# First expert layer: row products of the gathered tile spread otherwise over the routing stage, and the u products drawn out past the gates

## The chip, the core and the metric

One core of a Trainium2 chip runs the whole program in one launch. Its engines work side by side, each through its own queue of instructions in order: TensorE (PE), VectorE (DVE), ScalarE (ACT), GpSimd (POOL) and SyncE (SP, which here issues transfers only). Semaphores order them among each other. The metric is the device time of one execution in microseconds (us).

## The reference

Two blocks of two layers each. The change touches one place, the expert sublayer (`peer`) of layer 0 of the first block, which runs over 512 tokens (256 of the context, 256 of the latent sequence) with 1024 channels. There are 16384 experts, each a row of `u_tab` and a row of `v_tab`; a token uses 16 of them for each of 8 heads:

```
qry = (xb @ w_query).reshape(P, 8, 2, 128)
s = einsum('phcd,hckd->phck', qry, sub_keys)
top_s, top_i = top_k(s, 16)
cand_s = top_s[..., 0, :, None] + top_s[..., 1, None, :]      # 256 candidates of a head
best_s, pos = top_k(cand_s, 16)
gate = softmax(best_s)
act = gelu(einsum('pd,phkd->phk', xb, u_tab[idx]))
out = einsum('phk,phkd->pd', gate * act, v_tab[idx])
```

So for each token 128 rows of u are multiplied with the token's activations, and 128 rows of v are added up with the weights that come out.

## The kernel before, in words

The 512 tokens are four tiles of 128, and two ways of computing are mixed. **The chosen tile** (tile 0, class `Chosen`) does what the formula says: a step gathers one row of u for each of its 128 tokens (an indirect DMA on POOL, line 1295, 128 rows of 4 KB into one of four buffers `ch_r`) and DVE multiplies it with the token's activations and adds up (line 1311, one instruction and a short one that reads the sum). There are 128 such steps, here called row products, and later 128 more with rows of v (lines 1320 and 1322, `ch_y`). **The three dense tiles** (384 tokens, class `Experts`) multiply with every expert instead: 128 blocks of 128 experts, here called u products 0 to 127. For one block SP loads 0.5 MB of u (a transfer of 1 MB serves two blocks), ACT rounds it to `peer_uh` (line 1210), DVE takes the rest to `peer_ul` (line 1211), PE multiplies 24 times (lines 154 to 156), ACT applies the Gelu (line 1225) and the result is written to memory (`act_dram`). Experts that a token didn't choose get the gate 0. For that each dense tile makes a table of gates (`peer_gates`): for four tokens at a time ACT makes one-hots of the first key (lines 1171 and 1173), DVE one-hots of the second key times the gate (line 1180, four instructions, ten buffers), PE multiplies the two (line 1183) and ACT copies the result out (line 1184); every 32 tokens a block of it is written to memory (`g_dram`, line 1187). After that come the v products: SP loads gates (`gtile`) and activations, DVE and ACT make `coefh` and `coefl` and split v (`peer_vh`, `peer_vl`), PE multiplies.

Before its gates or its row products a tile goes through the router (`peer_route`): PE scores, and DVE's searches for the largest 16, then six operations of 128 x 2048 elements (`eq` and `key`).

The order of all this is set in three layers. `merge` runs several generators beside each other by a clock that each advances by the numbers it yields; `to(us, gen, own)` scales a generator so that it takes `us` in all; a u product advances its clock by `pace`. `routing()` is the list of stretches: router 0, then router 1 beside row products, then the gates of a dense tile beside the next router and row products, twice, then the last gates beside row products. The order in which the generators run is not yet the program's: a scheduler of the language orders each engine's instructions once more by its own estimate of durations, and keeps the order that `issue_after` (`K.behind`) asks for: instructions of the same engine in such a block come behind the one named. All buffers come from pools in which the next user waits for the last reader. The gathers' queue on POOL holds nothing else in this stage.

Of the kernel before, what the change touches and what calls it, by code (L numbers as in the profile page):

```python
# [1147 lines left out]
def peer_gates(K, pool, stage, t, route, g_d, scalar):  # L1148
# [3 lines left out]
    nc = K.nc  # L1152
# [11 lines left out]
    for c in range(128 // GT):  # L1164
        st = stage([128, 128, GT], c)
        for q in range(GT // 4):
# [10 lines left out]
            p = K.bank("v")  # L1177
            for k in range(4):
                o2 = pool.tile([128, 128], F32, name="oh2", tag="oh2", bufs=10)
                nc.vector.scalar_tensor_tensor(  # L1180
                    o2, K.iota, k2T[:, tk + k:tk + k + 1], gT[:, tk + k:tk + k + 1].to_broadcast([128, 128]),
                    op0=OP.is_equal, op1=OP.mult)
                nc.tensor.matmul(p[:, k * 128:(k + 1) * 128], o1[:, k], o2, start=True, stop=True)  # L1183
# [751 lines left out]
SEG = (1, 1, 0, 0)  # L1935
# [106 lines left out]
def peer_layer(K, A, tc, i, hT, hp, tag, nt, x, gate, ahead, pace, done, side=None, begin=None, chosen=0):  # L2042
# [5 lines left out]
    nc = K.nc  # L2048
    ntt = nt // 128
    spare = ntt == 2  # L2050
    dense = list(range(chosen, ntt))
    nd = nt - 128 * chosen
    g_d = K.dram.tile([nd // GT, 128, 128, GT], F32, name=f"g_dram{i}")
    act_d = K.dram.tile([ahead, 128, nd], F32, name=f"act_dram{i}")
    q_d = [K.dram.tile([128, 16, 128], F32, name=f"q_dram{i}{t}") for t in range(ntt)]
    with ExitStack() as c:
# [6 lines left out]
        with ExitStack() as c2:  # L2063
# [8 lines left out]
            gp = c2.enter_context(tc.tile_pool(name="gp", bufs=1, reuse_waits="tile"))  # L2072
            route = [[] for _ in range(ntt)]
# [18 lines left out]
            def to(us, gen, own):  # L2092
                return slow(gen, us / own)

            def rows(n, us):

                return to(us, (next(chs[0].go) for _ in range(n)), 1.7 * n)

            def gated(n):
                return peer_gates(K, gp, stage, n, route[dense[n]], g_d, chosen > 0)  # L2100

            def routing():
                if chosen:
                    yield from to(32, router(0), 73)
                    yield from merge(to(52, router(1), 73), rows(16, 52))
                    yield from merge(to(142, gated(0), 83), to(142, router(2), 73), rows(36, 142))
                    yield from merge(to(142, gated(1), 83), to(142, router(3), 73), rows(36, 142))
                    yield from merge(to(115, gated(2), 83), rows(40, 115))
                    return
                yield from router(0)  # L2110
                yield from merge(gated(0), router(1))
                yield from gated(1)
# [44 lines left out]
def program(ctx, tc, A, out):  # L2157
# [18 lines left out]
    with ExitStack() as c0:  # L2176
# [34 lines left out]
        late.close()  # L2211
        K.raw = raw
        N = Norm(K, None, x, lambda: hp.tile([128, 8, 512], F32, name="nxT", tag="plo", bufs=1))
        peer_layer(K, A, tc, 0, hT, hp, "ph", 512, x, SEG, 128, 3.77, N.raw, chosen=1)

        xl = x[2:4]
        h2 = hp.tile([128, 2, 8, 256], F32R, name="qhl", tag="ph", bufs=1)
# [198 lines left out]
```

## Time and profile before

| | |
|---|---|
| time, median of 3 runs | 4038.18 us (4034.49 to 4052.68) |
| the profiled execution's own time | 4038.09 us |
| its span | 4036.3 us |
| PE busy | 3756.6 us, 93% |
| DVE busy | 3067.0 us, 76% |
| ACT busy | 2110.7 us, 52% |
| POOL busy | 968.9 us, 24% |

The span runs from the first to the last instruction; what lies around it is the launch. A matmul counts as busy from its start to a modelled end, so a busy PE may still be slowed by its clock, which the profile gives as the share of full speed that was granted. The stage of the change, from the first u product to the first v product, lies between 985 and 1711 us.

### The profile page before, as it was taken

To read this page: it belongs to the slowest core of one execution; us is meant where nothing else is said; L and a number is where in the kernel's file an instruction comes from. 1 tells how busy PE (TensorE), PEld (TensorE's weight loads), DVE (VectorE), ACT (ScalarE), POOL (GpSimd) and SP (SyncE) were. 2 spreads that over 40 slices of the span, in tenths; PEclk is the share of its full clock that TensorE was granted. 3 is DMA by queue.
4 is the path that set the end of the run, shared out by engine and by line. 5 is a ranking of instruction groups with operands and counts; after the bars stand their busy time and mean duration, and the time that the engine had idled before them with its cause. 6 is when DMAs were issued, how large, how long until landed. Compare 5 with 4: busy or idle time off the path is not lost.

```text
span 4036.3 us, 61300 instructions
## 1 busy us (share of the span) xinstructions
PE 3756.6 (93%) x22031; PEld 3263.8 (81%) x22031; DVE 3067.0 (76%) x6258; ACT 2110.7 (52%) x3676; POOL 968.9 (24%) x1040
## 2 busy tenths in 40 slices
PE   7988987999999999899999889999999999988899
PEld 6868765788989899888888779999887768963697
DVE  6997578542999995487888757996677766859785
ACT  5545665533358677633333455665456545640364
POOL 1473255210144430033333300000000030115210
PEclk9999998999999999999999999999999989989999
DMA  4432554634599894699998247677689953542354
GB/s 175 159 115 87 165 175 152 199 133 161 200 322 337 316 346 176 221 386 358 353 355 315 97 141 242 234 255 260 229 303 315 327 178 126 182 172 84 127 188 157
DMA packets 359770, 890.37 MB, mean 221 GB/s; under 512 B 32568, under 2 KB 227752, under 8 KB 300584
## 3 DMA queue, kind: packets, MB, share of 16 engines
q1 hardware_dynamic: 237040, 614.87, 44.5%
q10 hardware_dynamic: 85560, 137.34, 9.3%
q0 software_dynamic: 36864, 134.23, 9.0%
q8 instruction: 173, 2.83, 0.3%
q14 instruction: 133, 1.09, 0.1%
HBM read 763.94 MB, written 122.39 MB: 220 GB/s over the span
## 4 chain that ended last, share of the span: by engine, by line
PE 58%; DVE 21%; DMA 11%; ACT 4%; issue 4%; POOL 3%; ACTq 0%; DVEq 0%; SPq 0%; POOLq 0%
PE ps_a L156 5%; PE ps_a L154 5%; PE ps_a L155 5%; PE ps_v L155 5%; PE ps_v L154 5%; PE ps_v L156 5%; PE ps_mm L155 3%; PE ps_mm L154 3%; PE ps_mm L156 3%; DMA act<-act_dram 3%; DMA ch_r<-in_peer_u_rows_dram,ch_i 3%; PE ps_v L1183 2%; DVE peer_ul L1211 2%; DMA wraw<-in_peer_v_dram 2%; DVE ch_r L1311 2%
## 5 line engine op out<-in xcount | busy, mean ns | idle before, releaser
L139 DVE TENSOR_TENSOR wlo<-wraw,whi 128x1024 fp32r<-128x1024 f32 x320 | 395.6, 1242 | 275.5 <-ACT whi L138 274.0
L155 PE MATMUL ps_v<-peer_vl,coefh 128*128 128x512 f32 x1280 | 501.9, 392 | 12.6 <-DVE peer_vl L1211 12.3
L154 PE MATMUL ps_v<-peer_vh,coefh 128*128 128x512 f32 x1280 | 491.8, 391 | 17.6 <-ACT coefh L1255 15.8
L138 ACT ACTIVATE whi<-wraw 128x1024 fp32r<-128x1024 f32 x324 | 340.7, 1058 | 316.2 <-PE ps_mm L155 73.8
L156 PE MATMUL ps_v<-peer_vh,coefl 128*128 128x512 f32 x1280 | 441.7, 390 | 0.0
L1210 ACT ACTIVATE peer_vh<-wraw 128x1024 fp32r<-128x1024 f32 x256 | 261.5, 1053 | 276.5 <-DMA wraw<-in_peer_v_dram 141.8
L1211 DVE TENSOR_TENSOR peer_vl<-wraw,peer_vh 128x1024 fp32r<-128x1024 f32 x256 | 306.7, 1222 | 121.5 <-ACT peer_vh L1210 121.4
L1210 ACT ACTIVATE peer_uh<-wraw 128x1024 fp32r<-128x1024 f32 x256 | 269.0, 1058 | 248.3 <-PE ps_a L155 184.9
L156 PE MATMUL ps_a<-ph,peer_ul 128*128 128x384 f32 x1024 | 354.7, 348 | 27.6 <-DVE peer_ul L1211 27.4
L1211 DVE TENSOR_TENSOR peer_ul<-wraw,peer_uh 128x1024 fp32r<-128x1024 f32 x256 | 311.5, 1223 | 79.9 <-ACT peer_uh L1210 78.4
L154 PE MATMUL ps_a<-ph,peer_uh 128*128 128x384 f32 x1024 | 355.0, 347 | 8.1 <-ACT peer_uh L1210 8.1
L155 PE MATMUL ps_a<-plo,peer_uh 128*128 128x384 f32 x1024 | 348.2, 340 | 0.0
L1295 POOL DMA_INDIRECT ch_r<-in_peer_v_dram,ch_i x128 | 198.7, 1552 | 506.9 <-DVE ch_y L1320 292.6
L155 PEld LDWEIGHTS ps_v<-peer_vl,coefh 128*128 128x128 f32 x1280 | 240.9, 188 | 68.7 <-DVE peer_vl L1211 19.4
L154 PEld LDWEIGHTS ps_v<-peer_vh,coefh 128*128 128x128 f32 x1280 | 240.4, 188 | 69.2 <-ACT coefh L1255 16.1
L154 PE MATMUL ps_a<-qhl,peer_uh 128*128 128x256 f32 x1024 | 290.3, 284 | 1.0 <-ACT act L1225 0.6
L156 PE MATMUL ps_a<-qhl,peer_ul 128*128 128x256 f32 x1024 | 289.0, 283 | 2.1 <-DVE peer_ul L1211 2.1
L155 PE MATMUL ps_a<-qhl,peer_uh 128*128 128x256 f32 x1024 | 289.2, 283 | 0.0
L1295 POOL DMA_INDIRECT ch_r<-in_peer_u_rows_dram,ch_i x128 | 184.1, 1438 | 406.1 <-DVE rep L1070 202.7
L156 PEld LDWEIGHTS ps_v<-peer_vh,coefl 128*128 128x128 f32 x1280 | 240.0, 188 | 48.8
L1180 DVE SCALAR_TENSOR_TENSOR oh<-iota,k2T,gT 128x128 f32<-128x128 f32 x640 | 192.8, 352 | 76.2 <-PE ps_v L1183 75.8
L156 PEld LDWEIGHTS ps_a<-ph,peer_ul 128*128 128x128 f32 x1024 | 196.4, 192 | 36.9 <-DVE peer_ul L1211 36.5
(681 smaller groups left out, 10348.0 us busy)
## 6 DMA issues: line engine op xcount, KB each, us to landing
wraw<-in_peer_u_dram SPq DMA_DIRECT2D x128, 1024.0 KB
wraw<-in_peer_v_dram SPq DMA_DIRECT2D x128, 1024.0 KB
wraw<-in_ffn_w_up_dram SPq DMA_DIRECT2D x44, 1024.0 KB
g_dram<-gst ACTq DMA_DIRECT2D x20, 2048.0 KB
ada_w<-in_ada_w_dram SPq DMA_DIRECT2D x136, 256.0 KB
wraw<-in_dn_w_in_dram SPq DMA_DIRECT2D x24, 1024.0 KB
act_dram<-act ACTq DMA_DIRECT2D x128, 192.0 KB
act<-act_dram SPq DMA_DIRECT2D x128, 192.0 KB
```

Of the source, the lines that this page charges most:

```text
L138: nc.scalar.activation(hi[:, :n], r, AF.Copy)
L139: (sub or nc.vector).tensor_tensor(lo[:, :n], r, f32v(hi[:, :n]), op=OP.subtract)
L154: nc.tensor.matmul(out, ah, bh, start=start, stop=False)
L155: nc.tensor.matmul(out, ah, bl, start=False, stop=False)
L156: nc.tensor.matmul(out, al, bh, start=False, stop=stop)
L1180: nc.vector.scalar_tensor_tensor(o2, K.iota, k2T[:, tk + k:tk + k + 1], gT[:, tk + k:tk + k + 1].to_broadcast([128, 128]), op0=OP.is_equal ...
L1183: nc.tensor.matmul(p[:, k * 128:(k + 1) * 128], o1[:, k], o2, start=True, stop=True)
L1210: nc.scalar.activation(hi, r, AF.Copy)
L1211: nc.vector.tensor_tensor(lo, r, f32v(hi), op=OP.subtract)
L1295: self.K.nc.gpsimd.indirect_dma_start(out=r, out_offset=None, in_=table, in_offset=bass.IndirectOffsetOnAxis(ap=self.idx[:, c:c + 1], axis=0))
L1311: nc.vector.tensor_tensor_reduce(out=r, in0=r, in1=self.h, scale=1.0, scalar=0.0, op0=OP.mult, op1=OP.add, accum_out=dots[:, c:c + 1])
```

## The change

Three things. The row products are dealt out otherwise over the stretches of `routing()`: 16, 36, 36 and 40 of them before (128 in all), 8, 26, 26 and 68 after. While gates are made, each row product is put behind the last one-hot on DVE that the gates' generator had made (`K.one_hot`, `K.gone`, `K.behind`); that binds DVE's instruction, not the gather on POOL. And a u product advances its generator's clock by 3.95 instead of 3.77 (units of that clock, not times); the five stretches of the routing add up to 483 of them, 128 u products to 483 before and to 506 after, so that some six of them come behind the end of the gates.

```diff
--- before.py
+++ after.py
@@ -1177,7 +1177,7 @@
             p = K.bank("v")
             for k in range(4):
                 o2 = pool.tile([128, 128], F32, name="oh2", tag="oh2", bufs=10)
-                nc.vector.scalar_tensor_tensor(
+                K.one_hot = nc.vector.scalar_tensor_tensor(
                     o2, K.iota, k2T[:, tk + k:tk + k + 1], gT[:, tk + k:tk + k + 1].to_broadcast([128, 128]),
                     op0=OP.is_equal, op1=OP.mult)
                 nc.tensor.matmul(p[:, k * 128:(k + 1) * 128], o1[:, k], o2, start=True, stop=True)
@@ -2094,18 +2094,27 @@
 
             def rows(n, us):
 
-                return to(us, (next(chs[0].go) for _ in range(n)), 1.7 * n)
+                def gen():
+                    for _ in range(n):
+                        with K.behind(*K.gone):
+                            w = next(chs[0].go)
+                        yield w
+                return to(us, gen(), 1.7 * n)
 
             def gated(n):
-                return peer_gates(K, gp, stage, n, route[dense[n]], g_d, chosen > 0)
+                for w in peer_gates(K, gp, stage, n, route[dense[n]], g_d, chosen > 0):
+                    K.gone = (K.one_hot,)
+                    yield w
+
+            K.gone = ()
 
             def routing():
                 if chosen:
                     yield from to(32, router(0), 73)
-                    yield from merge(to(52, router(1), 73), rows(16, 52))
-                    yield from merge(to(142, gated(0), 83), to(142, router(2), 73), rows(36, 142))
-                    yield from merge(to(142, gated(1), 83), to(142, router(3), 73), rows(36, 142))
-                    yield from merge(to(115, gated(2), 83), rows(40, 115))
+                    yield from merge(to(52, router(1), 73), rows(8, 52))
+                    yield from merge(to(142, gated(0), 83), to(142, router(2), 73), rows(26, 142))
+                    yield from merge(to(142, gated(1), 83), to(142, router(3), 73), rows(26, 142))
+                    yield from merge(to(115, gated(2), 83), rows(68, 115))
                     return
                 yield from router(0)
                 yield from merge(gated(0), router(1))
@@ -2211,7 +2220,7 @@
         late.close()
         K.raw = raw
         N = Norm(K, None, x, lambda: hp.tile([128, 8, 512], F32, name="nxT", tag="plo", bufs=1))
-        peer_layer(K, A, tc, 0, hT, hp, "ph", 512, x, SEG, 128, 3.77, N.raw, chosen=1)
+        peer_layer(K, A, tc, 0, hT, hp, "ph", 512, x, SEG, 128, 3.95, N.raw, chosen=1)
 
         xl = x[2:4]
         h2 = hp.tile([128, 2, 8, 256], F32R, name="qhl", tag="ph", bufs=1)
```

Where that puts the instructions, at three places. First DVE's queue in the middle of the last gates, around u product 102 (`peer_ul` is one u product's splitting, `oh` a one-hot, the two rows with `ch_d` one row product). Before:

```order
L1211 TENSOR_TENSOR peer_ul<-wraw,peer_uh 128x1024
L1180 SCALAR_TENSOR_TENSOR oh_15942<-iota,k2T,gT 128x128
L1180 SCALAR_TENSOR_TENSOR oh_15988<-iota,k2T,gT 128x128
L1180 SCALAR_TENSOR_TENSOR oh_15991<-iota,k2T,gT 128x128
L1180 SCALAR_TENSOR_TENSOR oh_15994<-iota,k2T,gT 128x128
L1211 TENSOR_TENSOR peer_ul<-wraw,peer_uh 128x1024
L1180 SCALAR_TENSOR_TENSOR oh_15997<-iota,k2T,gT 128x128
L1180 SCALAR_TENSOR_TENSOR oh_16050<-iota,k2T,gT 128x128
L1180 SCALAR_TENSOR_TENSOR oh_16053<-iota,k2T,gT 128x128
L1180 SCALAR_TENSOR_TENSOR oh_16056<-iota,k2T,gT 128x128
L1211 TENSOR_TENSOR peer_ul<-wraw,peer_uh 128x1024
```

After:

```order
L1211 TENSOR_TENSOR peer_ul<-wraw,peer_uh 128x1024
L1311 ISA ch_r,ch_d<-ch_r,ch_h 128x1024
L1311 ISA ch_d 128x1
L1211 TENSOR_TENSOR peer_ul<-wraw,peer_uh 128x1024
L1311 ISA ch_r,ch_d<-ch_r,ch_h 128x1024
L1311 ISA ch_d 128x1
L1211 TENSOR_TENSOR peer_ul<-wraw,peer_uh 128x1024
L1311 ISA ch_r,ch_d<-ch_r,ch_h 128x1024
L1311 ISA ch_d 128x1
L1180 SCALAR_TENSOR_TENSOR oh_16170<-iota,k2T,gT 128x128
L1311 ISA ch_r,ch_d<-ch_r,ch_h 128x1024
L1311 ISA ch_d 128x1
```

Where four one-hots stood between two u products, row products now stand too. Over the stage, counted on DVE between the `peer_ul` of u products 0, 20, 32, 88 and 127, the row products are 1, 19, 105 and 3 before (all 128 are done by product 127), and 0, 10, 50 and 63 after, with 5 more behind product 127. The one-hots there are 0, 0, 256 and 128 before, 0, 10, 246 and 128 after, and the routers' large operations 6, 4, 8 and 6 before, 6, 6, 12 and 0 after. The last one-hot stands ahead of `peer_ul` of product 127 before and of product 119 after.

Second, DVE's queue at the end of the stage, from the last two u products on (`ch_y` are the row products with v, `peer_vl` the splitting of v). Before:

```order
L1211 TENSOR_TENSOR peer_ul<-wraw,peer_uh 128x1024 x2
L1322 TENSOR_SCALAR ch_y<-ch_r,ch_d 128x1024
L1320 SCALAR_TENSOR_TENSOR ch_y<-ch_r,ch_d,ch_y 128x1024
L1211 TENSOR_TENSOR peer_vl<-wraw,peer_vh 128x1024 x2
L1320 SCALAR_TENSOR_TENSOR ch_y<-ch_r,ch_d,ch_y 128x1024
L1211 TENSOR_TENSOR peer_vl<-wraw,peer_vh 128x1024 x2
L1320 SCALAR_TENSOR_TENSOR ch_y<-ch_r,ch_d,ch_y 128x1024
L1252 TENSOR_TENSOR act<-act,gtile 128x384 x3
L1256 TENSOR_TENSOR coefl<-act,coefh 128x384 x3
```

After:

```order
L1211 TENSOR_TENSOR peer_ul<-wraw,peer_uh 128x1024 x2
L1211 TENSOR_TENSOR peer_vl<-wraw,peer_vh 128x1024
L1311 ISA ch_r,ch_d<-ch_r,ch_h 128x1024
L1311 ISA ch_d 128x1
L1211 TENSOR_TENSOR peer_vl<-wraw,peer_vh 128x1024
L1311 ISA ch_r,ch_d<-ch_r,ch_h 128x1024
L1311 ISA ch_d 128x1
L1311 ISA ch_r,ch_d<-ch_r,ch_h 128x1024
L1311 ISA ch_d 128x1
L1311 ISA ch_r,ch_d<-ch_r,ch_h 128x1024
L1311 ISA ch_d 128x1
L1252 TENSOR_TENSOR act<-act,gtile 128x384
```

Four of the last five row products now stand between the last u product and the first `act`, out of which the first coefficients are made.

Third, ACT's queue there (`g_dram` is the write of the last block of gates, `gate` a load that ACT issues for the end of the layer, `ch_d` the Gelu over all 128 row products). Before:

```order
L1225 ACTIVATE act<-ps_a 128x384
L1227 DMA act_dram_9320<-act 128x384
L1184 ACTIVATE gst<-ps_v 128x4x128
L1187 DMA g_dram_9319<-gst 128x4096
L1225 ACTIVATE act<-ps_a 128x384
L1227 DMA act_dram_9320<-act 128x384
L1225 ACTIVATE act<-ps_a 128x384
L1961 DMA gate<-ada_rows_146 128x1024
L1227 DMA act_dram_9320<-act 128x384
L1961 DMA gate<-ada_rows_146 128x1024
L1210 ACTIVATE peer_vh<-wraw 128x1024 x4
L1255 ACTIVATE coefh<-act 128x384 x4
```

After:

```order
L1210 ACTIVATE peer_uh<-wraw 128x1024 x2
L1210 ACTIVATE peer_vh<-wraw 128x1024
L1225 ACTIVATE act<-ps_a 128x384
L1210 ACTIVATE peer_vh<-wraw 128x1024
L1227 DMA act_dram_9320<-act 128x384
L1225 ACTIVATE act<-ps_a 128x384
L1961 DMA gate<-ada_rows_146 128x1024
L1227 DMA act_dram_9320<-act 128x384
L1961 DMA gate<-ada_rows_146 128x1024
L1210 ACTIVATE peer_vh<-wraw 128x1024 x2
L1255 ACTIVATE coefh<-act 128x384
L1314 ACTIVATE ch_d<-ch_d 128x128
```

The last write of gates is no longer among the last u products, two of the four first `peer_vh` stand ahead of the last Gelu, and the Gelu over the row products stands behind the first `coefh`; before it stood far ahead.

## Rows read from the trace of the kernel before

**Rows 1.** The stage cut in five: busy time of each engine, clock, DMA.

```profile
core 0: us, PE busy (x) PEld busy (x) DVE busy (x) ACT busy (x) POOL busy (x), PEclk, DMA share, GB/s
985.00:1094.00 109.00, 101.45 (x604) 98.83 (x602) 86.97 (x368) 39.45 (x56) 6.28 (x5) 0.99 0.54 188
1094.00:1153.00 59.00, 54.68 (x290) 52.22 (x290) 55.82 (x135) 19.54 (x28) 23.69 (x19) 0.95 0.89 308
1153.00:1491.00 338.00, 314.43 (x1921) 304.20 (x1922) 324.67 (x896) 250.25 (x506) 155.08 (x106) 0.97 0.90 330
1491.00:1695.00 204.00, 200.02 (x1222) 197.88 (x1220) 108.77 (x241) 144.86 (x275) 3.58 (x3) 0.98 0.54 198
1695.00:1711.00 16.00, 0.21 (x3) 0.03 (x1) 9.91 (x10) 4.98 (x7) 7.49 (x4) 0.67 0.99 354
```

**Rows 2.** What PE waited for, 1085 to 1711 us: total, times, longest.

```profile
PE ps_a L156 <- DVE peer_ul L1211: 23.2, 21, 3.7
PE ps_v L154 <- ACT coefh L1255: 15.8, 1, 15.8
PE ps_a L154 <- ACT peer_uh L1210: 8.1, 11, 1.9
```

**Rows 3.** Pieces of the chain: start, length in us up to the next.

```profile
1205.64 2.27 DVE peer_ul L1211 x2
...
1377.90 1.05 DVE oh L1180 x4
...
1394.38 1.14 DVE ch_r L1311
...
1506.35 2.20 DVE eq L1135
...
1689.07 11.69 DMA g_dram<-gst
```

**Rows 4.** Timeline where PE never waits: start, length in us, instruction.

```profile
1681.86 1.23 DVE L1211 TENSOR_TENSOR peer_ul<-wraw,peer_uh 128x1024 fp32r<-128x1024 f32 x1 [3.57 <-ACT peer_uh L1210]
...
1682.85 0.34 PE L155 MATMUL ps_a<-plo,peer_uh 128*128 128x384 f32 x1
...
1685.80 0.33 PE L154 MATMUL ps_a<-ph,peer_uh 128*128 128x384 f32 x1
...
1686.91 1.23 DVE L1211 TENSOR_TENSOR peer_ul<-wraw,peer_uh 128x1024 fp32r<-128x1024 f32 x1 [3.83 <-ACT peer_uh L1210]
```

**Rows 5.** One stretch in which PE never waits, columns as in rows 1.

```profile
1550.00:1600.00 50.00, 50.00 (x321) 50.00 (x320) 23.24 (x52) 41.44 (x81) 0.00 (x0) 1.00 0.51 182
```

**Rows 6.** Groups by line, 1153 to 1491 us: busy, mean ns, idle before.

```profile
L1295 POOL DMA_INDIRECT ch_r<-in_peer_u_rows_dram,ch_i x105 | 154.7, 1474 | 182.1 <-DVE ch_d L1311 75.8 <-DVE oh L1180 53.1 <-DVE rep L1070 12.4
...
L1311 DVE CUSTOM_DVE_ANT_0 ch_r<-ch_r,ch_h 128x1024 f32<-128x1024 f32 x105 | 126.7, 1222 | 13.3 <-DMA ch_r<-in_peer_u_rows_dram,ch_i 13.3
```

**Rows 7.** Tile ch_r, 1153 to 1491 us: POOL min, median, max; landings.

```profile
L1295 POOL DMA_INDIRECT ch_r<-in_peer_u_rows_dram,ch_i x105: 939/1360/3931, 1152.4 to 1484.5; - x105
...
DMA to landing us min/median/max: 4.3/7.0/15.8
```

**Rows 8.** DMA queue of the gathers, 985 to 1711 us: packets, MB, share.

```profile
q0 software_dynamic: 19237, 70.09, 27.4%
```

**Rows 9.** The other DMA queues, 1491 to 1695 us.

```profile
q1 hardware_dynamic: 3044, 21.27, 29.9%
q10 hardware_dynamic: 6360, 16.65, 21.0%
```

**Rows 10.** All DMA in the v products that follow, 1711 to 2204 us.

```profile
DMA packets 91370, 177.85 MB, mean 361 GB/s; under 512 B 5456, under 2 KB 67743, under 8 KB 83402
```

**Rows 11.** Group of the one-hots, 1491 to 1695 us, columns as in rows 6.

```profile
L1180 DVE SCALAR_TENSOR_TENSOR oh<-iota,k2T,gT 128x128 f32<-128x128 f32 x128 | 38.4, 348 | 72.9 <-PE ps_v L1183 72.9
```

**Rows 12.** Timeline of ACT at the change from u to v products.

```profile
1697.79 3.89 ACT L1210 ACTIVATE peer_vh<-wraw 128x1024 fp32r<-128x1024 f32 x4 [2.08 <-issue]
1710.40 0.99 ACT L1255 ACTIVATE coefh<-act 128x384 fp32r<-128x384 f32 x2 [8.72 <-DVE act L1252]
```

## Prediction

> **What bounds the kernel now.** I read the stage in which the change lies, 985 to 1711 us, in this order. First the busy time of each engine, cut where DVE has finished `peer_ul` of u products 20, 32 and 88, and at the end of PE's last u product [rows 1]. The reader is to see DVE at 325 of 338 us in the third stretch and PE at 200 of 204 us in the fourth: the bound moves from DVE to PE. All row products but one lie in the stretches in which DVE is the bound; in the fourth DVE works 109 of 204 us. Second, what PE waits for [rows 2]: 23.2 us for `peer_ul`, 8.1 us for `peer_uh`, and once 15.8 us, between the last u product and the first v product. Third, the chain that ended last, for the steps on DVE and for that last wait [rows 3]: the last block of gates is written to memory in 11.69 us from 1689, and only then can the gates be loaded. The stage could be better packed by some 45 us at most, 1.1% of the whole.
>
> The profiled execution took 4038.09 us around a span of 4036.3 us, and the median of the runs is 4038.18; I sum against 4038.1 and shift nothing.
>
> **Prices.** On DVE a step is its distance to the next: a row product 1.14 us, `peer_ul` 1.135, a one-hot 0.26, a router's large operation 2.2 [rows 3]. On PE a u product is 24 matmuls; 17 of them take 2.95 us where PE never waits, so 4.16 us for 24, and a u product with four one-hots takes 5.05, so 0.89 us for a group of four one-hots [rows 4].
>
> **Part 1: row products leave the third stretch (1153 to 1491).** By the counts in the section on the change, 55 of 105 row products leave it (55 x 1.14 = 63 us less on DVE) and ten one-hots (2.6 us); four large router operations come in earlier (8.8 us) with some 5 us of small ones around them. DVE's work falls from 324.7 to 273 us. PE's does not fall: 56 u products x 4.16 = 233 us, 62 groups of one-hots x 0.89 = 55 us, and some 7 us of router matmuls and transposes (an estimate from a price like the one-hots'), 295 us. ACT is busy 250 us now [rows 1] and keeps its work. So PE takes over as the bound, from 338 to something over 295 us. What is late next is PE's own pace. Its clock in this stretch was 0.97 of full speed, where it is 1.00 in a stretch without waits [rows 1, 5]. At 0.97 the 295 us are 304. Three more for short waits: the three engines stay close together, and DVE, when it was the bound, needed 338 us for 325 of work. I take 307, so 31 us less. Bounds: 295 (full clock, no wait) and 326 (7% lost on the 304, nearly twice the 4% that DVE loses now on its 325).
>
> The Trainium skill, on the page "TensorE: Matmul & The Clock Gate", section "A second HAM failure mode: psum-queue depth-cycling", says that a PE which idles briefly and often between groups of matmuls keeps switching between its clock's levels. The third stretch agrees with it, at 0.97 with short waits of the kind in [rows 2]; by that rule the 304 stand as long as any short waits are left, and without it the whole would be 3991.
>
> **Part 2: the first two stretches.** The first keeps its work but for one row product: 109 us, nothing gained (bounds 107 and 109). In the second (59 us) nine row products leave (10.3 us on DVE), ten one-hots (2.6) and two large router operations (4.4) come: 3.3 us less on DVE, which was busy 55.8 of 59. PE needs 12 x 4.16 + 3 groups, 53 us. I take 57, 2 us less (bounds 55 and 59).
>
> **Part 3: the row products arrive in the fourth stretch (1491 to 1695).** It gets 63, and two of the five behind the last u product, where three were: 65 gathers and some 65 x 1.14 = 74 us more on DVE, and loses the last router's large operations (6 x 2.2 = 13 us) and some 6 us around them. DVE goes from 109 to 164 us of 204. That stays hidden if it comes evenly. Behind a row product stand the one-hots and `peer_ul`, and for these PE waits; ahead of it now stands a one-hot, which waits for PE (72.9 us of such waits for 128 one-hots, harmless now [rows 11]). Gathers: POOL takes 1.47 us for one [rows 6], a landing 7.0 us in the middle [rows 7], the product 1.22 [rows 6], and there are four buffers: (1.47 + 7.0 + 1.22) / 4 = 2.4 us a row, where the stretch leaves 204 / 68 = 3.0. With the longest landing, 15.8 us [rows 7], it is 4.6. The DMA engines: the other queues were busy 29.9% and 21.0% of 204 us [rows 9], 104 us; the gathers' queue moved 70.09 MB, 134 gathers of 0.524 MB, in 27.4% of 726 us [rows 8], 1.49 us each; 104 + 65 x 1.49 = 200 us of 204. In bytes, 198 GB/s x 204 us [rows 1] plus 65 x 0.524 less the 1.6 MB of three gathers of v makes 73 MB, 358 GB/s. The v products hold 361 GB/s over 493 us [rows 10]. So DMA comes to the rate that it can hold, with little over. I take 208 us, 4 more than before. Bounds: 198 (PE's 40 x 4.16 + 33 x 0.89 us and its edges) and 250 (3.7 us a row, half way to the worst landing).
>
> **Part 4: six u products outlast the gates.** The last write of gates now leaves eight u products, over 33 us, before the end of the stretch, so its 11.69 us [rows 3] are hidden behind them. What is late next is ACT. Its queue at this place holds the last Gelu, two issues of `gate`, two `peer_vh`, then the first `coefh`. Before, ACT went on at 1697.79, 2.6 us after PE's end at 1695.2, and four `peer_vh` took 3.89 us [rows 12]; two are left: 2.6 + 1.95 + 0.5 for `coefh` (0.99 for two [rows 12]) is 5 us. On DVE six steps of 1.14 stand between the last `peer_ul` and the first `act`; `peer_ul` ended 7 us before PE [rows 4, 12], so the two come out together if the last gathers have landed. The second `coefh` now stands behind the Gelu over all row products, and that behind the last of them; the first v product covers this with some 4 us of matmuls. I take a wait of 7 us where 15.8 was: 9 us less (bounds 0 and 15 less).
>
> The v products themselves keep their work, and I leave them at their time; DVE's row products with v start a few us later. The scheduler also orders a few instructions of the attention layer and of later stages otherwise; I count that as 0, give or take 3.
>
> **Sum.** 0 - 2 - 31 + 4 - 9 = -38: 4038.1 - 38 = 4000 us.
>
> **The rivals.**
>
> *A, PE never waits.* The third stretch at 295 (-43), the fourth at 198 (-6), the last wait 1 us (-15), the second -2: 3972. For it: a stretch at clock 1.00 without any wait exists [rows 5]. Against it: DVE there had half its time free.
>
> *B, the gathers don't keep up in the fourth stretch.* DMA at its limit makes a landing 11 us long in the mean; 13.7 us over four buffers are 3.4 us a row, 65 x 3.4 = 221 us: 17 more than before. -2 - 31 + 17 - 6 (the tail of the row products is late for the v products too) = -22: 4016. For it: 200 of 204 us of DMA. Against it: 361 GB/s can be held [rows 10].
>
> *C, the change doesn't do what it says.* The third stretch is held up by the coupling of one-hots between ACT, DVE and PE and not by DVE's sum: 326 instead of 338 (-12), the fourth +4, the last wait -9, the second -2: 4019. For it: three engines at 250, 273 and 295 us. Against it: before, PE's waits are nearly all for `peer_ul` [rows 2].
>
> *D, slower.* The mechanism of B, at its far end: each row product that waits for its gather holds up the `peer_ul` behind it, and PE. The gains elsewhere are 42 us. The fourth stretch gives them all back at 246 us, 3.8 us a row, a mean landing of 12.5 us; at 13.7 us (4.1 a row, 267 us) the kernel is 21 us slower, 4059. With all landings at 15.8, 65 x 4.6 = 299, it would be 4091. For it: 15.8 us did occur at a DMA share of 0.90. Against it: the middle was 7.0 there [rows 1, 7].
>
> **How the numbers follow.** About 0.5% of the time, 20 us, can be told from no change. Chances: the forecast (3984 to 4014) 0.53, A 0.12, B 0.15, C 0.12, D 0.08. The likeliest is 4000. Faster than 4018: the forecast, A and a third of B's spread, 0.70 together; within 4018 to 4058: the rest of B and C, and D where it only gives the gain back, 0.23; slower 0.07. The range leaves out the far half of A and of D and a little of C: 3974 to 4034.
>
> **What the changed profile would show.** Right: PE busy and not DVE closest to the length of the third stretch, which shortens by some 30 us, and waits for `peer_ul` well under 23.2 us; DVE near 165 us and DMA near 1.0 in the fourth, which is as long as before; a wait of 5 to 9 us before the first v product, ended by `coefh`, with the last write of gates long done. Wrong: waits of DVE for gathers far over the 13.3 us of [rows 6], PE waiting for `peer_ul` in the fourth stretch (B, D); PE waiting for one-hots in the third (C); or a wait of 15 us still ahead of the first v product, then for a gather or for the Gelu over the row products.

## The result and the profile after

The changed kernel takes 3981.32 us in the median of 4 runs (3979.0 to 3982.66), beside 4036.7 for the kernel before: a ratio of 0.9861, 95% interval [0.9847, 0.9876]. The profiled execution took 3981.17 us around a span of 3979.4, 56.9 us less than the one of before. The forecast was 4000 with a range from 3974 to 4034: the sign and the range held, and the gain was half as large again as the 38 us of the sum. The 3981.32 lies 3 us below the span that the forecast itself was given (3984 to 4014) and 7 us above the lower end of the range. Between the profiled executions 51.9 of the 56.9 us lie in the stage of the change.

The stage cut at the same places as in [rows 1] (columns as there):

```profile
982.00:1084.00 102.00, 98.97 (x592) 96.65 (x591) 84.10 (x359) 38.03 (x54) 1.43 (x2) 1.00 0.51 175
1084.00:1141.00 57.00, 55.77 (x330) 55.01 (x328) 55.27 (x140) 26.52 (x43) 14.67 (x13) 1.00 0.78 281
1141.00:1434.50 293.50, 293.50 (x1891) 293.04 (x1890) 276.18 (x837) 249.34 (x499) 70.29 (x50) 1.00 0.79 284
1434.50:1645.30 210.80, 202.84 (x1229) 198.94 (x1227) 153.38 (x294) 138.36 (x267) 84.18 (x63) 0.99 0.93 346
1645.30:1656.10 10.80, 0.00 (x0) 0.00 (x0) 8.00 (x12) 5.29 (x7) 4.46 (x3) 0.67 0.86 300
```

The reader is to see the third row. PE is busy for the whole 293.50 us, at a clock of 1.00: the stretch was 338 us long, with DVE at its limit and the clock at 0.97. The next row shows the price, DMA at 0.93 and PE short of the stretch by 8 us. What PE waits for, 1075 to 1657 us, in the form of [rows 2]:

```profile
PE ps_v L154 <- ACT coefh L1255: 10.8, 1, 10.8
PE ps_a L154 <- ACT peer_uh L1210: 5.9, 9, 2.1
PE ps_a L156 <- DVE peer_ul L1211: 3.3, 5, 1.0
```

23.2 us of waits for `peer_ul` have become 3.3. DVE's own waits, first in the third stretch, then in the fourth up to the first v product:

```profile
DVE peer_ul L1211 <- ACT peer_uh L1210: 9.7, 10, 3.3
...
DVE ch_r L1311 <- DMA ch_r<-in_peer_u_rows_dram,ch_i: 21.1, 13, 4.1
DVE peer_ul L1211 <- ACT peer_uh L1210: 19.0, 10, 3.3
DVE oh L1180 <- PE ps_v L1183: 10.3, 9, 2.4
DVE peer_vl L1211 <- ACT peer_vh L1210: 9.7, 1, 9.7
```

And ACT's in the third:

```profile
ACT peer_uh L1210 <- PE ps_a L155: 36.0, 24, 3.4
```

In the third stretch the 13.3 us of waits for gathers of [rows 6] are gone, and DVE now waits for ACT, which waits for PE: PE sets the pace. In the fourth DVE waits 21.1 us for gathers. The tile `ch_r` there, beside [rows 7]:

```profile
L1295 POOL DMA_INDIRECT ch_r<-in_peer_u_rows_dram,ch_i x64: 939/1081/1990, 1437.0 to 1650.7; - x64
...
DMA to landing us min/median/max: 5.0/7.8/14.9
```

And the end of the stage: the writes of gates (their issue on ACT's queue), then ACT's and DVE's timelines from the last u products on.

```profile
L1187 ACTq DMA_DIRECT2D g_dram<-gst x2: 326/326/327, 1570.7 to 1612.3; - x2
```

```profile
1647.02 1.06 ACT L1210 ACTIVATE peer_vh<-wraw 128x1024 fp32r<-128x1024 f32 x1 [10.05 <-DMA wraw<-in_peer_v_dram]
...
1655.55 0.52 ACT L1255 ACTIVATE coefh<-act 128x384 fp32r<-128x384 f32 x1 [2.88 <-DVE act L1252]
```

```profile
1636.05 2.36 DVE L1211 TENSOR_TENSOR peer_ul<-wraw,peer_uh 128x1024 fp32r<-128x1024 f32 x2 [1.55 <-ACT peer_uh L1210]
1648.10 1.22 DVE L1211 TENSOR_TENSOR peer_vl<-wraw,peer_vh 128x1024 fp32r<-128x1024 f32 x1 [9.69 <-ACT peer_vh L1210]
...
1654.96 0.55 DVE L1252 TENSOR_TENSOR act<-act,gtile 128x384 f32<-128x384 f32 x1
```

The last write of gates is issued at 1612.3, 33 us ahead of PE's last u product: the 11.69 us of [rows 3] are hidden, as forecast. Late in its place is the first load of v. SP issued it only at 1630.86, ACT's first `peer_vh` waited 10.05 us for it, and DVE, with nothing but `peer_vl` next in its queue, stood 9.7 us. Its row products and the first `act` came behind that.

### The profile page after: what moved, and what is told of

It reads as the page before. It is cut to its first block, busy times and chain, and to the rows that moved or that the text cites. A ratio compares the mean times of both kernels' runs of the same rounds, so it can differ in the third digit from the quotient of the medians.

```text
span 3979.4 us, 61280 instructions
## 1 busy us (share of the span) xinstructions
PE 3729.4 (94%) x22031; PEld 3243.2 (82%) x22031; DVE 3065.4 (77%) x6258; ACT 2107.4 (53%) x3676; POOL 975.9 (25%) x1040
## 5 line engine op out<-in xcount | busy, mean ns | idle before, releaser
L156 PE MATMUL ps_v<-peer_vh,coefl 128*128 128x512 f32 x1280 | 402.3, 391 | 0.0
L1295 POOL DMA_INDIRECT ch_r<-in_peer_u_rows_dram,ch_i x128 | 172.3, 1346 | 586.5 <-DVE topi L1072 194.2
L1295 POOL DMA_INDIRECT ch_r<-in_peer_v_dram,ch_i x128 | 217.3, 1698 | 296.0 <-DVE ch_y L1320 274.3
L1184 ACT ACTIVATE gst<-ps_v 128x512 f32<-128x512 f32 x160 | 179.9, 1124 | 62.6 <-PE ps_v L1183 62.1
L1180 DVE SCALAR_TENSOR_TENSOR oh<-iota,k2T,gT 128x128 f32<-128x128 f32 x640 | 192.5, 345 | 14.1 <-PE ps_v L1183 13.4
```

The lines of the kernel that those rows point to most:

```text
L156: nc.tensor.matmul(out, al, bh, start=False, stop=stop)
L1180: K.one_hot = nc.vector.scalar_tensor_tensor(o2, K.iota, k2T[:, tk + k:tk + k + 1], gT[:, tk + k:tk + k + 1].to_broadcast([128, 128]), op0 ...
L1184: nc.scalar.activation(st[:, :, q * 4:q * 4 + 4].rearrange("p a k -> p k a"), p.rearrange("p (k a) -> p k a", k=4), AF.Copy)
L1295: self.K.nc.gpsimd.indirect_dma_start(out=r, out_offset=None, in_=table, in_offset=bass.IndirectOffsetOnAxis(ap=self.idx[:, c:c + 1], axis=0))
```

## The experiments

Each ran beside the kernel before on its own chip. Stretches are measured in the profiled execution, between the same ends as in [rows 1]: the ends of `peer_ul` 32 and 88 on DVE, PE's last u product, PE's first v product. "Stage" is from the first u product to the first v product, so it holds the first and second stretch too, which the table leaves out. The cuts at `peer_ul` are DVE's: how far PE lies behind DVE there moves time from one stretch to the next, the stage not. In the second column E is the edge that puts row products behind one-hots, P the pace of 3.95, C the new counts, and "late" the row products dealt to the last part, 68 in the change.

| run | edits | median us | ratio to before, 95% | third | fourth | last wait | stage |
|---|---|---|---|---|---|---|---|
| before | none | | | 337.5 | 204.2 | 15.8 | 725.9 |
| the change | E P C | 3981.3 | 0.9861 [0.9847, 0.9876] | 293.7 | 210.8 | 10.8 | 674.0 |
| change_again | E P C | 3987.8 | 0.9879 [0.9863, 0.9895] | 293.7 | 209.7 | 9.1 | 671.2 |
| behind_only | E | 3996.9 | 0.9903 [0.9878, 0.9929] | 311.4 | 197.1 | 16.4 | 687.8 |
| pace_only | P | 4024.5 | 0.9979 [0.9964, 0.9994] | 336.6 | 206.9 | 13.0 | 720.7 |
| no_pace | E C | 4016.7 | 0.9955 [0.9939, 0.9972] | 304.9 | 220.6 | 21.6 | 708.8 |
| old_counts | E P | 3987.0 | 0.9889 [0.9873, 0.9906] | 313.1 | 197.7 | 13.4 | 686.1 |
| less_late | E P, 54 late | 4000.6 | 0.9921 [0.9906, 0.9936] | 308.8 | 213.6 | 8.4 | 690.6 |
| mid | E P, 60 late | 3993.7 | 0.9893 [0.9876, 0.991] | 303.8 | 222.2 | 8.9 | 693.6 |
| pace_4_10 | E C, 4.10 | 3990.4 | 0.9893 [0.9877, 0.991] | 301.0 | 217.4 | 8.5 | 686.0 |
| v_first | E P C, v load | 3982.6 | 0.9867 [0.9844, 0.989] | 293.7 | 216.2 | 12.1 | 681.7 |
| half_rows | E P C, half u rows | 3974.7 | 0.984 [0.9824, 0.9857] | 299.0 | 206.1 | 13.3 | 673.6 |
| before_half | half u rows | 4018.0 | 0.9967 [0.9953, 0.9981] | 320.5 | 203.9 | 16.2 | 710.2 |
| before_half_8 | half u rows, 8 in flight | 4008.1 | 0.9943 [0.9917, 0.9969] | 310.1 | 204.5 | 16.5 | 700.3 |

The rest of the program, the same code but for a few rows of order, spreads by up to 17 us from one profiled execution to the next (from the last v product to the end 1787.0 us in old_counts, 1804.1 in change_again), so the stage tells two runs apart better than the whole does.

### Which of the three edits

Two combinations make no program of their own: compiled, the counts alone leave all five engines' instructions in exactly the order of before, and counts with pace in that of pace alone. The scheduler undoes the dealing-out unless the edge holds it.

**behind_only**, the edge without the new counts and pace:

```diff
-rows(8, 52)  rows(26, 142)  rows(26, 142)  rows(68, 115)
+rows(16, 52) rows(36, 142)  rows(36, 142)  rows(40, 115)
-peer_layer(K, A, tc, 0, hT, hp, "ph", 512, x, SEG, 128, 3.95, N.raw, chosen=1)
+peer_layer(K, A, tc, 0, hT, hp, "ph", 512, x, SEG, 128, 3.77, N.raw, chosen=1)
```

> The row products are bound behind the one-hots, but dealt out 16, 36, 36 and 40 and with the pace 3.77, as before. In DVE's order 72 of them then stand in the third stretch (105 before, 50 in the change) and 40 in the fourth. Theory 1 (what counts is DVE's sum in the third stretch, and PE's 294 us are its floor): DVE is busy 276 us there in the change, 22 products and 10 one-hots more make 304, so the third stretch takes 304 to 310 us; the gates end at u product 125, so the wait ahead of the v products stays at 11 to 14 us; 4002 to 4012 in all. Theory 2 (the place of the products behind the one-hots is what frees PE, not their number in the stretch): third stretch at 294 to 298 us, 3990 to 3995 in all. Theory 3 (the gain comes from the u products' pace): 4030 or more.

The edge alone brings 0.97% of the change's 1.2 to 1.4%. Theory 1 comes nearest: 311.4 us for the third stretch, 1 above its 304 to 310. The whole is 5 us under its 4002 to 4012, since the fourth stretch falls too (204.2 to 197.1), and theory 2's 294 to 298 and theory 3's 4030 are far off. Third and fourth stretch:

```profile
1144.00:1455.50 311.50, 304.87 (x1927) 300.16 (x1926) 304.32 (x892) 255.14 (x511) 97.00 (x72) 0.99 0.85 309
1455.50:1652.60 197.10, 197.10 (x1228) 196.74 (x1226) 132.28 (x251) 139.85 (x270) 58.68 (x40) 1.00 0.82 290
```

Held behind one-hots that aren't there yet, 40 row products slide into the fourth stretch by themselves, and PE is busy there all the time. The last wait stays, since gates and u products still end together.

**pace_only**, the kernel before with 3.95 for 3.77:

> The pace 3.95 alone; no binding, 16, 36, 36 and 40. DVE's order has 102 row products in the third stretch and 7 in the fourth; the last one-hot stands ahead of u product 120. Theory 1: third stretch 330 to 337 us as before; the first product's gather no longer stands in the first stretch (5 us less there); the wait ahead of the v products falls from 15.8 to 5 to 10; 4020 to 4030 in all. Theory 3 (the pace brings the gain): 3981 to 3990.

0.2%, and 5 us of the stage, as theory 1 had it. They don't come from the u products behind the gates: the first stretch loses 7 us with the row product that leaves it, the last wait only 3 (13.0; 5 to 10 were expected), the second and fourth gain 3 each, and the third stretch stays at 336.6 us.

**no_pace**, the change with 3.77:

> The change without its pace (3.77): binding and 8, 26, 26, 68. DVE's order has the same 50 products in the third stretch, and the last one-hot stands ahead of u product 123 instead of 119. Theory 1: third stretch 294 us as in the change; the last gates' write of some 12 us is just hidden or nearly so, the wait ahead of the v products 10 to 14 us; 3980 to 3987 in all, at most 6 above the change. Theory 3: 4010 or more.

Theory 1 failed here. The time is in theory 3's region (4010 or more), though pace_only has shown that the pace alone doesn't bring the gain. More than half of what the edge alone gains is lost:

```profile
1141.00:1446.00 305.00, 299.92 (x1904) 298.02 (x1903) 276.70 (x834) 249.75 (x498) 66.70 (x50) 0.99 0.76 273
1446.00:1667.00 221.00, 207.16 (x1243) 204.60 (x1241) 153.60 (x297) 142.07 (x274) 83.41 (x63) 0.96 0.85 312
```

```profile
DVE ch_r L1311 <- DMA ch_r<-in_peer_u_rows_dram,ch_i: 30.7, 11, 7.0
...
ACT ch_d L1314 <- DVE ch_d L1311: 9.5, 1, 9.5
```

DVE's work is that of the change to within 0.6 us in both stretches (276.70 and 153.60), and yet they are 11 and 10 us longer. So DVE's sum doesn't settle the time alone. In the third, most of the 11 us is work that PE brings along: at the end of `peer_ul` 32 the Gelu of that u product starts 13.3 us later, in the change 5.4 us later, and between the Gelus of u products 32 and 88 it is 298.9 us where the change takes 295.5. In the fourth stretch the waits for gathers are 30.7 us instead of 21.1, the gates end with the u products, and the Gelu over the row products, which waits 9.5 us for the last of them, stands ahead of the first `coefh`: a last wait of 21.6 us.

**old_counts**, the edge and the pace, the counts of before:

```diff
-rows(8, 52)  rows(26, 142)  rows(26, 142)  rows(68, 115)
+rows(16, 52) rows(36, 142)  rows(36, 142)  rows(40, 115)
```

> The change with one part undone: the row products are dealt out as before (16, 36, 36, 40), with the edge to the one-hots and the pace of 3.95 kept. The order has 72 row products in the third stretch, 40 in the fourth, as with the edge alone; the last one-hot stands ahead of u product 119. What the counts are worth beside the other two parts is the question. Theory 1 (the third stretch is set by the larger of DVE's sum and PE's 294 us): DVE has 22 row products more than with the change there, some 25 us, 301 us of work, so a stretch of 308 to 312 us; the fourth 197 to 204; the last wait 9 to 12 us, since the gates still end ahead of the u products: 3987 to 4000 us. Theory 2 (what gains is that the gates end ahead of the u products, and the counts add nothing): within 5 us of the change's own 3981 to 3988.

In the whole it is not told apart from the change (3987.0; the change 3981.3 and 3987.8): that is theory 2's number. By stretches it is theory 1's: 313.1 and 197.7, a stage 12 to 15 us longer, which the shorter rest of the profiled execution covers. What the counts add is thus some 0.3 to 0.4% by the stage, and these runs don't show it in the whole time.

Counts and pace belong together. With the edge in place, the stage grows by 21 us when the new counts come without the pace (687.8 to 708.8) and shrinks by 12 to 15 when they come with it (686.1 to 674.0 and 671.2). The pace brings 2 us of stage with the old counts (687.8 to 686.1) and 35 to 38 with the new ones. Each of these stages is one profiled execution; the two of the change differ by 2.8 us.

### How many row products, and what DVE's sum says

**less_late** and **mid**, the change with other counts:

```diff
-rows(8, 52)  rows(26, 142)  rows(26, 142)  rows(68, 115)
+rows(10, 52) rows(32, 142)  rows(32, 142)  rows(54, 115)
```

```diff
-rows(8, 52)  rows(26, 142)  rows(26, 142)  rows(68, 115)
+rows(8, 52)  rows(30, 142)  rows(30, 142)  rows(60, 115)
```

> The change with 10, 32, 32 and 54 row products instead of 8, 26, 26 and 68. In DVE's order 66 stand in the third stretch (50 in the change), 52 in the fourth (63) and none behind the last u product (5). DVE's sum in the third stretch is 276 + 16 x 1.14 + some one-hots = 296 to 298 us, PE's 294. Theory A (DMA holds up the end): third stretch 298 to 304, fourth 198 to 203, wait 5 to 8; 3972 to 3980, a little under the change. Theory B: third stretch 298 to 304, fourth 207 or more, the wait as in the change; 3985 to 3995.

> The same with 8, 30, 30 and 60: 62 row products in the third stretch, 56 in the fourth, none behind the last u product; the last one-hot ahead of u product 117 instead of 119. Theory A: third stretch 294 to 300 (DVE's sum 290 to 293), fourth 199 to 204, wait 5 to 8; 3968 to 3977. Theory B: fourth 207 or more and the wait 10 or more; 3980 to 3990.

**pace_4_10**, the change with 4.10 for 3.95:

> The change with a pace of 4.10 instead of 3.95: the u products are due later still, the last one-hot stands ahead of u product 115 instead of 118, 58 row products stand in the third stretch (with the change 50) and 57 in the fourth (63). Theory 1 (DVE's sum or PE's, whichever is larger): DVE in the third stretch some 276 + 9 = 285 us, still under 294, so a stretch of 294 to 300 us; the fourth 204 to 210; the last wait as short as with the change, since the v load sets it, 8 to 11 us: 3976 to 3990 us, no different from the change. Rival (three engines so near to each other hold each other up, as where 62 and 66 row products stood there): 303 to 309 us in the third stretch, and 3990 to 4000 us.

Neither theory holds as it stands. 301.0 us lies between theory 1's 294 to 300 and the rival's 303 to 309, and 3990.4 at the border of the two (3976 to 3990 and 3990 to 4000); the fourth stretch took 217.4 us, not 204 to 210. less_late and mid took longer in the third stretch (308.8 and 303.8) than the 298 to 304 and 294 to 300 expected of them, and longer in the whole than either theory. In the fourth they have theory B's 207 or more (213.6 and 222.2), so fewer row products on DVE don't shorten it. The third stretches of the three, in the order less_late, mid, pace_4_10:

```profile
1141.00:1450.00 309.00, 305.30 (x1954) 302.40 (x1954) 299.20 (x885) 256.83 (x512) 84.69 (x66) 1.00 0.83 302
```

```profile
1142.00:1445.50 303.50, 299.61 (x1922) 297.75 (x1921) 292.62 (x870) 257.01 (x516) 77.14 (x62) 1.00 0.83 298
```

```profile
1144.00:1445.00 301.00, 299.62 (x1929) 298.05 (x1927) 290.03 (x871) 257.35 (x519) 69.28 (x57) 1.00 0.81 292
```

DVE lies some 10 us under each length (299.2 in 309, 292.6 in 303.5, 290.0 in 301), but in all three PE is busier than DVE: 305.3, 299.6 and 299.6 us, with 3.7, 3.9 and 1.4 us on top. So the 294 us of PE that the expectations went by is not PE's floor in these runs. With the row products, one-hots move too: 261, 256 and 264 of them stand in this stretch, 246 in the change, where PE's 293.5 us are the whole length with DVE at 276.2. In less_late PE also brings work along, as in no_pace (11.2 us behind DVE at the first cut). By the order 52, 56 and 57 row products stand in the fourth stretch, where the change has 63, and it is no shorter for that: 213.6, 222.2 and 217.4 us. POOL works on 61, 63 and 60 gathers there (the first of v among them), the change on 63.

### Is it DVE's sum, or where the row products stand

**before_half** and **before_half_8**, the kernel before with half of each u row:

```diff
 r = self.pool.tile([128, 1024], F32, name="ch_r", tag="ch_r", bufs=4)
+if table is self.u:
+    r, table = r[:, :512], self.half
...
-in0=r, in1=self.h,
+in0=r, in1=self.h[:, :512],
```

In the second a buffer holds two of these halves:

```diff
+if table is self.v or c % 2 == 0:
+    self.r = self.pool.tile([128, 1024], F32, name="ch_r", tag="ch_r", bufs=4)
+r = self.r
...
+    r = r[:, c % 2 * 512:c % 2 * 512 + 512]
```

> The kernel before with 512 of each gathered row's 1024 channels read and multiplied for the u rows, so that a row product costs DVE some 0.6 us instead of 1.14 (this leaves half of the dot products out). 98 row products stay in the third stretch. Theory 1 (DVE's sum of 325 us set that stretch): DVE falls by some 98 x 0.5 = 50 us to 275, and the stretch from 338 to 294 to 300 us at a clock of 1.00, with no part of the change made; the last wait stays at some 16 us: about 3990 us. The rival (the place of the row products in the order, behind one-hots and ahead of peer_ul, holds PE up, not DVE's sum): the stretch stays above 320 us, and the clock at 0.97.

> The run of the kernel before with half of each u row (half of the dot products left out), now with two half rows in each of the four buffers, so that up to eight gathers can be on their way instead of four. The order still has 90 row products in the third stretch, in bunches, and no part of the change is made. With four in flight that stretch took 320.5 us at a clock of 0.97: DVE worked 277.8 us, waited 26.6 us for gathers in its bunches and 12.4 us for PE. Theory 1 (the bunches drain the buffers, the next row product waits for its gather, and peer_ul and PE wait behind it): with eight in flight DVE's waits for gathers there fall under 10 us, PE's waits for peer_ul from 19.3 us to under 10, and the stretch comes to 296 to 308 us: some 4000 us. The rival (a bunch holds PE up by its own work alone, five row products between two peer_ul, whether the rows are there or not): the stretch stays at 315 to 322 us, the clock at 0.97: 4012 to 4020 us.

before_half took DVE's work in the third stretch to the change's own figure and left the order nearly as it was:

```profile
1148.00:1468.50 320.50, 300.04 (x1855) 296.06 (x1856) 277.82 (x925) 234.00 (x465) 123.42 (x98) 0.97 0.76 262
```

```profile
PE ps_a L156 <- DVE peer_ul L1211: 19.3, 9, 4.5
...
DVE ch_r L1315 <- DMA ch_r<-in_peer_u_rows_dram,ch_i: 26.6, 13, 5.9
```

277.8 us of work on DVE, and the stretch is 320.5 us long, at 0.97: the rival's numbers. 47 us less of work gave 17 us. DVE now waits 26.6 us for gathers, and PE for the `peer_ul` behind them. With eight gathers in flight:

```profile
1152.00:1461.50 309.50, 296.06 (x1850) 290.85 (x1849) 278.81 (x909) 237.25 (x473) 108.74 (x88) 0.99 0.72 254
```

```profile
PE ps_a L156 <- DVE peer_ul L1211: 7.5, 7, 1.8
...
DVE ch_r L1317 <- DMA ch_r<-in_peer_u_rows_dram,ch_i: 8.6, 7, 3.0
```

Both waits fell under 10 us, as theory 1 had it, the clock came to 0.99, and the stretch lost 10.4 us more (310.1; 296 to 308 were expected, so it fell a little short). So the waits for gathers cost some 10 us of it; the two orders aren't quite the same (98 and 89 row products in the stretch), but DVE's work is, to within 1 us. The waits come where row products are crowded: in before_half 54 of the 98 begin within 2.4 us of the last one, the pace that the prediction worked out for four buffers; in the kernel before 45 of 104, in behind_only 17 of 72, in the change 4 of 50. Half rows halve two things at once, DVE's work and the bytes of a gather, and no run takes them apart here.

### The fourth stretch and the last wait

**half_rows**, the change with the first of the two diffs above (half of the dot products left out):

> The change with half of each row of u gathered and multiplied (512 of 1024 channels; the chosen tile's result is not the reference's). DVE's order has about the same numbers: 49 row products in the third stretch, 68 in the fourth. Theory A (the fourth stretch and the wait behind it are held up by DMA at its limit, 346 GB/s and a share of 0.93 in the change): 68 x 0.26 MB less, so the fourth stretch falls from 211 to its floor on PE, 197 to 200, and the wait from 10.8 to 4 to 6; 3960 to 3967 in all. Theory B (they are held up by the order in which row products, one-hots and splittings stand on DVE, in which PE's and DVE's instructions wait for each other): the fourth stretch stays at 207 or more and the wait at 9 or more; 3975 or more.

The profile is against the bytes. Fourth stretch and last wait are 206.1 and 13.3 us, together 219.4 where the change takes 221.6 and 218.8; that is theory B's wait (9 or more) and its 207 to within 1 us. The waits for gathers didn't go:

```profile
DVE ch_r L1315 <- DMA ch_r<-in_peer_u_rows_dram,ch_i: 28.1, 17, 4.3
...
DMA to landing us min/median/max: 3.6/6.3/13.3
```

(The landings take in 16 gathers of v with whole rows; for the 64 of u alone the median is 5.9 us.) The whole time is against that reading: 3974.7, 13 us under change_again, which ran on the same chip, with intervals that don't meet. The profiled execution was the longest of the five (3989.4), so it doesn't show where those 13 us lie. That stays open.

**v_first**, the first load of v ahead of the gate loads in SP's queue:

```diff
+v = ()
+if first and e0 == 0:
+    r = K.raw.tile([128, 2048], F32, name="wraw", tag="wraw")
+    v = (nc.sync.dma_start(r, self.A["peer_v"][self.i][:, 0:2048]),)
+    self.raw["peer_v", 0] = r
+with K.behind(*v):
     nc.sync.dma_start(g.rearrange("p c e k -> p c (e k)"), ...
```

> The change, with the first load of v issued ahead of the first load of gates on SP. In the changed kernel the wait ahead of the first v product ended like this: ACT's first peer_vh waited 10.0 us for that load, which SP had issued behind two loads of gates, and the last Gelus stood behind it. Theory 1 (the load's place in the queue makes that wait): 10.8 us fall to 4 to 6 and the second wait of 2.8 to under 1; 3972 to 3977 in all. Rival (the load is late because the DMA engines are full, whatever its place; the gates then come late instead): the wait stays at 9 to 11, 3980 to 3983.

No gain: the load, though first, was issued at 1632.3, later than the change's 1630.86, and the wait was 12.1 us behind a fourth stretch of 216.2. ACT's first `peer_vh` no longer waited 10 us, but the first `act` came only at 1662.23, after DVE had stood 4.9 us. As I read it, a second chain, from the last Gelu (1651.29) through memory to `act`, is about as long as the one that was shortened; the profile names no releaser for that wait, so it isn't shown. The wait and the whole are near the rival's (9 to 11 and 3980 to 3983), but its ground, full DMA engines, has no run of its own; the gate loads were issued later, from 1632.7 where the change has 1625.1.

**change_again**, the change once more, on the chip of less_late, mid and half_rows:

> The change itself once more, on the chip and beside the runs of the next three. 3975 to 3990, by the same shares: third stretch 293 to 296 us, fourth 208 to 216, wait ahead of the v products 10 to 13.

Its third stretch has the 293.7 us and the clock of 1.00 of the first time. The wait of 9.1 us is a little under the 10 to 13 expected.

## Why the prediction was right, step by step

**First stretch, 0 forecast, -7 measured** (109.2 to 101.9 us). I counted one row product of 1.14 us. It took its wait for the gather with it, 4.1 us ahead of `peer_ul`, so 5.2 of the 7 us. Every run with a pace of 3.95 or 4.10 shows 102 us and every run with 3.77 shows 109, so it is the pace that moves this row product, and not the counts.

**Second, -2 forecast, -2.3 measured.**

**Third, -31 forecast, -44 measured.** This is the mis-sized term, 13 of the 19 us that the sum was short. The mechanism (DVE's load falls under PE's, PE becomes the bound at 295) was right for the change: PE is busy 293.50 of 293.50 us. Wrong was that I kept the clock of 0.97 (9 us) and 3 us of waits. Neither was a property of the stretch. Both went together with a DVE that was late: its 324 us of work and the 13.3 us of waits for gathers make up the whole 338, and PE waited for `peer_ul` behind them. Rival A's 295 for this stretch was the right value; its 198 and 1 for the next two were not. And the argument by DVE's sum alone was too simple: before_half has the sum without the order and is still 27 us longer than the change. Half rows (half of DVE's price, and half of a gather's bytes) gave 17 us there and eight gathers in flight 10 more; the last 16 us down to 294 go with the change's order and pace, and no run splits them further. The change itself keeps whole rows and four buffers, so these runs show what was at work before, and are no shares of the change's own gain.

The Trainium skill, "TensorE: Matmul & The Clock Gate", section "A second HAM failure mode: psum-queue depth-cycling", describes a PE that idles briefly and often between groups of matmuls and keeps switching its clock. From it I had taken that the 304 would stand as long as any short waits were left. The change leaves none in this stretch, so it doesn't test that; old_counts does, with waits for `peer_ul` left and a clock of 1.00:

```profile
1142.40:1455.50 313.10, 303.90 (x1930) 298.17 (x1929) 304.24 (x891) 254.98 (x513) 92.97 (x72) 1.00 0.84 308
```

```profile
PE ps_a L156 <- DVE peer_ul L1211: 6.6, 8, 1.7
```

Eight waits of at most 1.7 us cost their own 6.6 us and not the clock, so the rule as I had used it was too strict. The Trainium skill speaks of frequent idle times there, and I had read any. In the kernel before, over 1153 to 1491 us, 17 such waits went with a clock of 0.97:

```profile
PE ps_a L156 <- DVE peer_ul L1211: 16.7, 17, 2.2
```

Whether their number, their length or their sum makes the difference, these runs don't tell.

**Fourth, +4 forecast, +6.6 measured.** DVE was forecast at 164 us and shows 153, DMA near 1.0 and shows 0.93; DVE waits 21.1 us for gathers, more than the 13.3 of [rows 6], and PE stands still for 8 us in all. Rivals B and D saw the danger: no_pace and mid, with as many gathers there (63), took 10 to 11 us more at a clock of 0.95 to 0.96, DVE waiting 30.7 and 26.9 us for gathers. That the gathers make it is not shown, since half_rows waits 28.1 us for them and takes 206.1.

**Last wait, -9 forecast, -5.0 measured.** The write of gates is hidden and `coefh` ends the wait, as the step said. It takes 10.8 us, not 7, since the four `peer_vh` didn't find their data: the load of v, which I had taken to be there, came some 10 us late, and DVE's row products stood behind it.

**Behind it, 0 forecast.** The second `coefh` comes at 1664.19, behind the Gelu over the row products, and PE waits 2.8 us for it, which I had thought covered: v products 528.7 us instead of 525.8. The remaining -8 us lie before the stage (-3.0) and after the v products (-5.0); change_again has +4.6 in the latter, so they are spread and no gain of the change. Without them the gain is 49 us against the 38 forecast. The two terms that were too small (first and third stretch, 20 us together) outweigh the three that were too good (fourth stretch, last wait and v products, some 10 us).

**What was not foreseen** is which edit does the work: the counts, from which I had worked out 63 us less on DVE, are ignored by the scheduler unless the edge holds them, the edge brings most of the gain with the old counts too, and edge and counts without the pace lose more than half of it. By the traces the last one-hot stands ahead of u product 126 before and 118 after, each one earlier than in the section on the change, which moves no term of the sum.

## What to carry to other kernels

When an engine looks full, split its stretch into work and waits before pricing a change by the work: in the kernel before, halving each row product's work and bytes gave 17 us where the change gives 44, and letting the gathers arrive gave 10 more and most of the clock (0.97 to 0.99). Where a change has several edits, look at the order that each makes alone, because one of them may be what lets the others act. Count the work of every engine again in the order that comes out: I went on with PE's 294 us where other counts had brought it to 300 and more. The stretches with the edge and a clock of 0.99 to 1.00 ran 0 to 9 us in 300 beyond the busiest engine. Look also for the loads that are late once a wait ahead of them is hidden.

## What the runs showed that was not expected

A gather of half the bytes lands little sooner: 5.9 us in the middle for 0.26 MB (half_rows), 7.8 for 0.52 MB (the change), in the same stretch (DMA at 0.86 and 0.93). If all of the 1.9 us were due to the bytes, half of the 7.8 us would still not be; that is an estimate from these two medians.

The issue of a transfer on SP is not always short. Around the first loads of gates and of v, two issues of each took 5.66 and 8.84 us, where one before them took 0.33; in each pair one issue is long (5.23 and 8.36 us) and the other 0.38:

```profile
1621.49 0.33 SPq L1205 DMA_DIRECT2D wraw<-in_peer_u_dram  x1
1625.14 5.66 SPq L1246 DMA_DIRECT2D gtile<-g_dram  x2
1630.86 8.84 SPq L1205 DMA_DIRECT2D wraw<-in_peer_v_dram  x2
```

Whatever stands next in that queue is late by as much. In v_first the load of v, issued ahead of the gates, took 0.33 us, and the long issues came again with the gates (8.88 us) and the loads of v behind them (4.55 us). None of the runs separates what holds the issue up.
